# An encoder layer with expert retrieval: the v stage set up two blocks ahead, gathers spread over the whole stage

## The chip, the cores and the metric

One core of one Trainium2 chip. The metric is the device time of one execution in microseconds (us). The engines are named as the profile names them: PE is TensorE (with PEld for its weight loads), DVE is VectorE, ACT is ScalarE, POOL is GpSimd, and SP is SyncE, whose instruction stream here holds almost nothing but DMA issues (SPq). Each engine works through its own instructions strictly in order.

## The reference

One encoder layer, run on two sequences that share the weights: a prompt of 256 tokens and a sample of 512 tokens, model width 1024. After a norm and a projection come a banded attention and a dilated attention, gated, merged and added to x. Then follows the expert layer, where the change is:

```python
def peer(h, w_query, sub_keys_1, sub_keys_2, expert_u, expert_v):
    ...
    v1, i1 = lax.top_k(s1, PEER_TOPK)
    v2, i2 = lax.top_k(s2, PEER_TOPK)
    ...
    idx = (e1 * PEER_KEYS + e2).reshape(T, PEER_HEADS * PEER_TOPK)
    g = jax.nn.softmax(top, axis=-1).reshape(T, PEER_HEADS * PEER_TOPK)
    ...
        u = expert_u[ic]
        a = jax.nn.gelu(jnp.einsum('ted,td->te', u, tc, preferred_element_type=jnp.float32), approximate=False)
        vv = expert_v[ic]
        return jnp.einsum('te,ted->td', (gc * a).astype(tc.dtype), vv)
```

Each token picks 128 of 16384 experts (8 heads, 16 each) with gate weights g. A chosen expert gives gelu(u . h) times its gate, and that many times its row of expert_v is added to x. All is float32.

## The kernel before

**Products.** A float32 operand is split into two parts in the fast matmul format: `split` (L138) writes hi, a cast on ACT (L139), and lo = src - hi, a subtraction on DVE (L140). `mm3` (L143) then makes three matmuls: hi x hi (L144), lo x hi (L145), hi x lo (L146).

**The sample's expert layer is computed densely**, over all 16384 experts in 128 blocks of 128. `gbuild` builds the matrix of gates from one-hot products and stores it to gd in DRAM. The **u stage** (`stage1`, L730) loads a block of expert_u (ur, 512 KB), splits it into uh and ul, makes 24 matmuls against the 512 tokens (tTh, tTl) into pu, applies gelu on ACT (ga_) and stores that (256 KB, issued by ACT) to ad in DRAM. It runs woven into `gbuild`. The **v stage** (`dense`, L743) runs after it: per block, `stage2` (L748) issues on SP the load of vr (a block of expert_v, 512 KB) and of gl (the block's gelu, 256 KB), and for every eighth block gt (gates of eight blocks, 2 MB); it splits vr into vh and vl, multiplies gl by gt on DVE (L761) and splits that into ph and pl. The block's 24 matmuls add into eight banks, held0 to held7 (two halves of four token tiles), which collect over all 128 blocks. Block 122 also loads xe, the residual (2 MB, L774); after the last block each bank is added to xe on DVE (L782) and stored to y (L783).

**The prompt's expert layer is gathered.** `gather` (L790) makes, for each of two tiles of 128 tokens, 128 indirect DMAs of rows of expert_u (512 KB each, issued by POOL, L799, into buffers gr), each with a product and sum against the token on DVE (L806), then 128 of expert_v, each added into x on DVE by its weight (L814): 512 gathers in all. The second tile's x is x5, stored to y (L815) when its last sum is done.

**The order.** The program is written as generators that are woven together: `fill` and `weave` (L818, L827) run one step of the gathers whenever the main work has collected enough "due"; the paces are GB in the build stage and GV in the v stage, in gathers per unit (a block of the v stage yields 0.5 twice). A gather carries a wait called "pace" on `anchor[0]`, the cast or gelu on ACT that was issued last when it was written. From this program a scheduler, which plans with a timeline of its own, sets a fixed order on each engine. Tiles come from pools with a set number of buffers (bufs); a new tile in a buffer waits for the readers of the tile that was there. The pool of the v stage (L842 and below, named dv, from the right side of the memory) is opened when the u stage's pool is closed, and may take its place; then its first tiles wait for what used that memory.

Of the kernel before, what the change touches and what calls it, by code (L numbers as in the profile page):

```python
# [30 lines left out]
SYNC = mybir.DependencyInfo(mybir.DependencyClass.Sync, mybir.DependencyReason.DATA)  # L31
FILL = 2.25
# [12 lines left out]
GB, GV = (2.4, 2.0)  # L45
# [3 lines left out]
def tile_peer(ctx: ExitStack, tc: tile.TileContext, a: dict):  # L49
# [93 lines left out]
    def mm3(out, lh, ll, rh, rl, first, last):  # L143
        pe.matmul(out, lhsT=lh, rhs=rh, start=first, stop=False)  # L144
        pe.matmul(out, lhsT=lh, rhs=rl, start=False, stop=False)  # L145
        pe.matmul(out, lhsT=ll, rhs=rh, start=False, stop=last)  # L146
# [596 lines left out]
    def dense(pv_, psd):  # L743
# [4 lines left out]
        def stage2(j):  # L748
            g, b = divmod(j, GRP)
            if b == 0:  # L750
                gts[g] = pv_.tile([128, S_S // GCH, GRP, GCH], F32, tag="gt", name="gt", bufs=2)
                nc.sync.dma_start(gts[g], gd[:, :, g * GRP:(g + 1) * GRP, :].rearrange("c p e t -> p c e t"))
            vr = pv_.tile([128, D], F32, tag="vr", name="vr", bufs=5)
            nc.sync.dma_start(vr, vrows[j])
            ga = pv_.tile([128, S_S], F32, tag="gl", name="gl", bufs=4)
            nc.sync.dma_start(ga, ad[j])
            vh = pv_.tile([128, D], F32R, tag="vh", name="vh", bufs=3)
            vl = pv_.tile([128, D], F32R, tag="vl", name="vl", bufs=3)
            split(vh, vl, vr)
            gv = ga.rearrange("p (c t) -> p c t", t=GCH)  # L760
            ve.tensor_tensor(gv, gv, gts[g][:, :, b, :], op=ALU.mult)  # L761
            ph = pv_.tile([128, S_S], F32R, tag="ph", name="ph", bufs=3)
            pl = pv_.tile([128, S_S], F32R, tag="pl", name="pl", bufs=3)
            anchor[0] = split(ph, pl, ga)
            return ph, pl, vh, vl

        nxt = stage2(0)
        for j in range(128):
            ph, pl, vh, vl = nxt
            if j < 127:  # L770
                nxt = stage2(j + 1)
# [4 lines left out]
            for i in range(8):  # L776
# [3 lines left out]
                mm3(held[i], ph[:, c], pl[:, c], vh[:, cs], vl[:, cs], j == 0, j == 127)  # L780
                if j == 127:
                    ve.tensor_tensor(x[t][:, cs], held[i], x[t][:, cs], op=ALU.add)  # L782
                    nc.sync.dma_start(a["y"][t * 128:(t + 1) * 128, cs], x[t][:, cs])  # L783
# [180 lines left out]
```

## Time and profile before

| what | value |
|---|---|
| time, three runs | 2470.12, 2473.23, 2475.72 us (median 2473.23) |
| profiled execution, device time | 2468.71 us |
| its span | 2466.9 us |
| PE busy | 2350.8 us (95%), 11926 matmuls |
| PEld busy | 1964.5 us (80%) |
| DVE busy | 1886.5 us (76%) |
| ACT busy | 1076.1 us (44%) |
| POOL busy | 812.1 us (33%) |
| DMA | 642.79 MB, mean 261 GB/s |

The span is the stretch of the trace; the device time holds 1.8 us around it. Times in the rows are in us from the start of the span. The u stage ends at about 1725 us and the v stage fills the rest. A matmul row has a modelled end, so matmuls are best counted by their starts. In a row of the windows the engines come in the order PE, PEld, DVE, ACT, POOL, and PEclk is the granted clock of PE as a share of full speed. In a timeline row the value in brackets is how long the engine had been idle before, and what released it.

### The profile page before, as it was taken

To read this page: it belongs to the slowest core of one execution; us is meant where nothing else is said; L and a number is where in the kernel's file an instruction comes from. 1 tells how busy PE (TensorE), PEld (TensorE's weight loads), DVE (VectorE), ACT (ScalarE), POOL (GpSimd) and SP (SyncE) were. 2 spreads that over 40 slices of the span, in tenths; PEclk is the share of its full clock that TensorE was granted. 3 is DMA by queue.
4 is the path that set the end of the run, shared out by engine and by line. 5 is a ranking of instruction groups with operands and counts; after the bars stand their busy time and mean duration, and the time that the engine had idled before them with its cause. 6 is when DMAs were issued, how large, how long until landed. Compare 5 with 4: busy or idle time off the path is not lost. (4 is left out here: it accounts for less than half of the span.)

```text
span 2466.9 us, 34172 instructions
## 1 busy us (share of the span) xinstructions
PE 2350.8 (95%) x11926; PEld 1964.5 (80%) x11926; DVE 1886.5 (76%) x4013; ACT 1076.1 (44%) x1848; POOL 812.1 (33%) x624
## 2 busy tenths in 40 slices
PE   8998998999998999999999999997999999999999
PEld 6787877877887888888888888876888777777777
DVE  6765699677688889978579889853787888789873
ACT  5764435434433344367466666732222222222222
POOL 0000320345555401044144544420444443444310
PEclk9999999989998999999999999999999999999999
DMA  6423542467787434479789999995899999999972
GB/s 214 145 87 128 179 136 73 151 224 224 271 280 262 137 107 137 152 289 370 250 305 372 358 352 341 339 375 211 322 392 368 343 349 352 356 353 371 376 268 103
DMA packets 246365, 642.79 MB, mean 261 GB/s; under 512 B 22576, under 2 KB 77488, under 8 KB 244144
## 3 DMA queue, kind: packets, MB, share of 16 engines
q1 hardware_dynamic: 151728, 305.02, 36.4%
q0 software_dynamic: 73728, 268.47, 30.0%
q10 hardware_dynamic: 20736, 67.12, 6.8%
q8 instruction: 94, 1.54, 0.3%
q14 instruction: 79, 0.65, 0.1%
HBM read 561.60 MB, written 77.59 MB: 259 GB/s over the span
## 5 line engine op out<-in xcount | busy, mean ns | idle before, releaser
L799 POOL DMA_INDIRECT gr<-u,pidx x256 | 329.0, 1285 | 558.9 <-ACT ph L139 168.1
L799 POOL DMA_INDIRECT gr<-v,pidx x256 | 333.4, 1302 | 459.9 <-ACT ph L139 196.2
L144 PE MATMUL held<-vh,ph 128*128 128x512 f32 x1024 | 403.0, 394 | 31.3 <-ACT ph L139 30.7
L144 PE MATMUL pu<-tTh,uh 128*128 128x512 f32 x1024 | 407.4, 398 | 14.2 <-ACT uh L139 14.2
L146 PE MATMUL pu<-tTh,ul 128*128 128x512 f32 x1024 | 401.3, 392 | 4.1 <-DVE ul L140 4.1
L806 DVE SCALAR_TENSOR_TENSOR gr<-gr,tok 128x1024 f32<-128x1024 f32 x256 | 330.8, 1301 | 96.7 <-DMA gr<-u,pidx 96.5
L145 PE MATMUL held<-vl,ph 128*128 128x512 f32 x1024 | 400.8, 391 | 0.0
L145 PE MATMUL pu<-tTl,uh 128*128 128x512 f32 x1024 | 400.6, 391 | 0.0
L814 DVE SCALAR_TENSOR_TENSOR x<-gr,act,x 128x1024 f32<-128x1024 f32 x256 | 327.4, 1279 | 42.5 <-DMA gr<-v,pidx 40.6
L146 PE MATMUL held<-vh,pl 128*128 128x512 f32 x1024 | 314.9, 389 | 0.0
L144 PEld LDWEIGHTS held<-vh,ph 128*128 128x128 f32 x1024 | 193.9, 189 | 78.3 <-ACT ph L139 37.2
L140 POOL TENSOR_TENSOR wlo<-wraw,whi 128x1024 fp32r<-128x1024 f32 x51 | 128.6, 2522 | 376.8 <-ACT whi L139 373.8
L139 ACT CAST vh<-vr 128x1024 fp32r<-128x1024 f32 x128 | 134.5, 1051 | 257.0 <-PE held L146 154.2
L144 PEld LDWEIGHTS pu<-tTh,uh 128*128 128x128 f32 x1024 | 193.8, 189 | 53.2 <-ACT uh L139 15.9
L140 DVE TENSOR_TENSOR vl<-vr,vh 128x1024 fp32r<-128x1024 f32 x128 | 156.5, 1222 | 102.4 <-ACT vh L139 98.4
L146 PEld LDWEIGHTS pu<-tTh,ul 128*128 128x128 f32 x1024 | 193.3, 189 | 46.2 <-DVE ul L140 6.1
L145 PEld LDWEIGHTS held<-vl,ph 128*128 128x128 f32 x1024 | 193.8, 189 | 40.0
L146 PEld LDWEIGHTS held<-vh,pl 128*128 128x128 f32 x1024 | 192.2, 188 | 40.0
L145 PEld LDWEIGHTS pu<-tTl,uh 128*128 128x128 f32 x1024 | 193.5, 189 | 37.6
L139 ACT CAST whi<-wraw 128x1024 fp32r<-128x1024 f32 x137 | 143.8, 1050 | 167.7 <-DMA wraw<-w_in 52.7
L139 ACT CAST uh<-ur 128x1024 fp32r<-128x1024 f32 x128 | 133.8, 1050 | 175.7 <-PE pu L145 92.7
L139 ACT CAST ph<-gl 128x512 fp32r<-128x512 f32 x128 | 79.4, 620 | 267.0 <-DVE gl L761 106.5
(400 smaller groups left out, 4565.5 us busy)
## 6 DMA issues: line engine op xcount, KB each, us to landing
ur<-ublk SPq DMA_DIRECT2D x128, 512.0 KB
vr<-v SPq DMA_DIRECT2D x128, 512.0 KB
wraw<-w_in SPq DMA_DIRECT2D x80, 512.0 KB
gd<-gs ACTq DMA_DIRECT2D x16, 2048.0 KB
gt<-gd SPq DMA_DIRECT2D x16, 2048.0 KB
gl<-ad SPq DMA_DIRECT2D x128, 256.0 KB
wraw<-w_query SPq DMA_DIRECT2D x32, 512.0 KB
wraw<-w_out SPq DMA_DIRECT2D x16, 512.0 KB
```

The lines of the kernel that those rows point to most:

```text
L139: i = ac.copy(hi, src)
L140: eng.tensor_tensor(lo, src, hi.bitcast(F32), op=ALU.subtract)
L144: pe.matmul(out, lhsT=lh, rhs=rh, start=first, stop=False)
L145: pe.matmul(out, lhsT=lh, rhs=rl, start=False, stop=False)
L146: pe.matmul(out, lhsT=ll, rhs=rh, start=False, stop=last)
L799: st = gp.indirect_dma_start(out=g, out_offset=None, in_=tab, in_offset=bass.IndirectOffsetOnAxis(ap=pidx[t][:, s:s + 1], axis=0))
L806: ve.scalar_tensor_tensor(g, g, 1.0, tok, op0=ALU.mult, op1=ALU.mult, accum_out=act[:, s:s + 1])
L814: ve.scalar_tensor_tensor(xt, g, act[:, s:s + 1], xt, op0=ALU.mult, op1=ALU.add)
```

## The change

`stage2` is called two blocks ahead of the matmuls instead of one: the parts of blocks 0 and 1 are set up first, then in turn block j+2 before the matmuls of block j. vh, vl, ph and pl have four buffers each instead of three, vr has four instead of five. GB goes from 2.4 to 2.3 and GV from 2.0 to 1.75. In the last block each bank's three matmuls are tied to come behind those of the bank before (a dependency that sets the scheduler's order and puts no wait into the program). Line numbers shift by one to seven.

```diff
--- before.py
+++ after.py
@@ -29,6 +29,7 @@
 CAND = [16 // (i + 1) for i in range(16)]
 NCAND = sum(CAND)
 SYNC = mybir.DependencyInfo(mybir.DependencyClass.Sync, mybir.DependencyReason.DATA)
+ORDERED = mybir.DependencyInfo(mybir.DependencyClass.NoSync, mybir.DependencyReason.DATA)
 FILL = 2.25
 FG = 2.25
 FL = {"p": 1, "s": 3}
@@ -42,7 +43,7 @@
 PGP, PGS = (0.5, 0.45)
 ORDER, SLB = ('pppbpbbb', 3)
 U0, UP, UB = (8, 0.45, 1.0)
-GB, GV = (2.4, 2.0)
+GB, GV = (2.3, 1.75)
 
 
 @with_exitstack
@@ -141,9 +142,10 @@
         return i
 
     def mm3(out, lh, ll, rh, rl, first, last):
-        pe.matmul(out, lhsT=lh, rhs=rh, start=first, stop=False)
-        pe.matmul(out, lhsT=lh, rhs=rl, start=False, stop=False)
-        pe.matmul(out, lhsT=ll, rhs=rh, start=False, stop=last)
+        a_ = pe.matmul(out, lhsT=lh, rhs=rh, start=first, stop=False)
+        b_ = pe.matmul(out, lhsT=lh, rhs=rl, start=False, stop=False)
+        c_ = pe.matmul(out, lhsT=ll, rhs=rh, start=False, stop=last)
+        return a_, b_, c_
 
     def norm_tok(pool, xt, g, dst, ssq=None):
 
@@ -750,25 +752,26 @@
             if b == 0:
                 gts[g] = pv_.tile([128, S_S // GCH, GRP, GCH], F32, tag="gt", name="gt", bufs=2)
                 nc.sync.dma_start(gts[g], gd[:, :, g * GRP:(g + 1) * GRP, :].rearrange("c p e t -> p c e t"))
-            vr = pv_.tile([128, D], F32, tag="vr", name="vr", bufs=5)
+            vr = pv_.tile([128, D], F32, tag="vr", name="vr", bufs=4)
             nc.sync.dma_start(vr, vrows[j])
             ga = pv_.tile([128, S_S], F32, tag="gl", name="gl", bufs=4)
             nc.sync.dma_start(ga, ad[j])
-            vh = pv_.tile([128, D], F32R, tag="vh", name="vh", bufs=3)
-            vl = pv_.tile([128, D], F32R, tag="vl", name="vl", bufs=3)
+            vh = pv_.tile([128, D], F32R, tag="vh", name="vh", bufs=4)
+            vl = pv_.tile([128, D], F32R, tag="vl", name="vl", bufs=4)
             split(vh, vl, vr)
             gv = ga.rearrange("p (c t) -> p c t", t=GCH)
             ve.tensor_tensor(gv, gv, gts[g][:, :, b, :], op=ALU.mult)
-            ph = pv_.tile([128, S_S], F32R, tag="ph", name="ph", bufs=3)
-            pl = pv_.tile([128, S_S], F32R, tag="pl", name="pl", bufs=3)
+            ph = pv_.tile([128, S_S], F32R, tag="ph", name="ph", bufs=4)
+            pl = pv_.tile([128, S_S], F32R, tag="pl", name="pl", bufs=4)
             anchor[0] = split(ph, pl, ga)
             return ph, pl, vh, vl
 
-        nxt = stage2(0)
+        nxt = [stage2(0), stage2(1)]
+        prev = None
         for j in range(128):
-            ph, pl, vh, vl = nxt
-            if j < 127:
-                nxt = stage2(j + 1)
+            ph, pl, vh, vl = nxt.pop(0)
+            if j < 126:
+                nxt.append(stage2(j + 2))
             if j == 122:
                 xe = pv_.tile([128, 4, D], F32, tag="gt", name="xe", bufs=2)
                 nc.sync.dma_start(xe, xs.rearrange("(t p) d -> p t d", p=128))
@@ -777,8 +780,12 @@
                 t, n = divmod(i, 2)
                 c = slice(t * 128, t * 128 + 128)
                 cs = slice(n * 512, n * 512 + 512)
-                mm3(held[i], ph[:, c], pl[:, c], vh[:, cs], vl[:, cs], j == 0, j == 127)
+                ms = mm3(held[i], ph[:, c], pl[:, c], vh[:, cs], vl[:, cs], j == 0, j == 127)
                 if j == 127:
+                    if prev is not None:
+                        for m in ms:
+                            tc.add_manual_dep(m.ins, prev.ins.name, ORDERED, reason="output by output")
+                    prev = ms[2]
                     ve.tensor_tensor(x[t][:, cs], held[i], x[t][:, cs], op=ALU.add)
                     nc.sync.dma_start(a["y"][t * 128:(t + 1) * 128, cs], x[t][:, cs])
                 if i % 4 == 3:
```

How the instructions stand then on the engines, at three places.

**ACT, v stage, blocks 81 to 86 of before.** vh and ph are the casts of split; the numbers only tell tiles apart. In the order of blocks these rows are ph81, vh83, ph82, vh84, vh85, ph83, vh86, ph84, ph85:

```order
L139 CAST ph_20132<-gl_20125 128x512
L139 CAST vh_20213<-vr_20209 128x1024
L139 CAST ph_20175<-gl_20168 128x512
L139 CAST vh_20256<-vr_20252 128x1024
L139 CAST vh_20299<-vr_20295 128x1024
L139 CAST ph_20218<-gl_20211 128x512
L139 CAST vh_20342<-vr_20338 128x1024
L139 CAST ph_20261<-gl_20254 128x512
L139 CAST ph_20304<-gl_20297 128x512
```

The same place after; in the order of blocks vh81, ph81, vh82, vh83, vh84, ph82, ph83, ph84, vh85, ph85:

```order
L140 CAST vh_20013<-vr_20009 128x1024
L140 CAST ph_20018<-gl_20011 128x512
L140 CAST vh_20056<-vr_20052 128x1024
L140 CAST vh_20096<-vr_20092 128x1024
L140 CAST vh_20139<-vr_20135 128x1024
L140 CAST ph_20061<-gl_20054 128x512
L140 CAST ph_20101<-gl_20094 128x512
L140 CAST ph_20144<-gl_20137 128x512
L140 CAST vh_20182<-vr_20178 128x1024
L140 CAST ph_20187<-gl_20180 128x512
```

Before, vh85 stands ahead of ph83 and vh86 ahead of ph84: two blocks ahead, with three buffers. After, three vh stand in a row, then three ph; vh84 stands two blocks ahead of ph82, with four buffers, and no vh stands three blocks ahead of a ph.

**SP, from the u stage to the v stage, before.** ur is a block of the u stage, gt, vr and gl are the loads of the v stage; behind a row stands what it waits for (DMAHW and DMASW are transfers, the others engines):

```order
L732 DMA ur_16314<-ublk 128x1024 [waits DMAHW0_49,DVE_49]
L752 DMA gt_16641<-gd_91 128x16x256 [waits DMAHW5_49,DMAHW1_49,PE_49]
L754 DMA vr_16643<-v 128x1024 [waits DMAHW6_49]
L756 DMA gl_16645<-ad_95 128x512 [waits PE_49]
L754 DMA vr_16656<-v 128x1024
L756 DMA gl_16658<-ad_95 128x512 [waits DMASW4_49,DMASW5_49,DMASW3_49,DMASW6_49,DMASW2_49,DMASW7_49,DMASW1_49,DMAHW1_49,DMASW0_49,DVE_49]
L754 DMA vr_16699<-v 128x1024 [waits DMAHW3_49]
```

Six more ur, down to that of block 127, stand further down this queue, behind thirteen more loads of the v stage. After:

```order
L734 DMA ur_16494<-ublk 128x1024 [waits DMAHW3_49,DVE_49]
L734 DMA ur_16528<-ublk 128x1024 [waits DMAHW4_49,DVE_49]
L734 DMA ur_16562<-ublk 128x1024 [waits DMAHW6_49,DMAHW2_49,DVE_49]
L754 DMA gt_16617<-gd_91 128x16x256 [waits DMAHW4_49,DMAHW5_49,DMAHW3_49,DMAHW6_49,DMAHW1_49,DMAHW7_49,DMAHW0_49,Activation_49]
L756 DMA vr_16619<-v 128x1024 [waits DMAHW2_49]
L758 DMA gl_16621<-ad_95 128x512
L756 DMA vr_16632<-v 128x1024
L758 DMA gl_16634<-ad_95 128x512
```

The last ur stands ahead of every load of the v stage now, and the first gt waits for eight semaphores: the last gelu of the u stage (ga_ of block 127) and the last seven stores of ga_ to ad. The v stage's pool is 8 KB per partition larger, and the first gt now lies on the memory of ga_.

**DVE, at the end of the program, before.** xe is the residual, held3 to held7 the last banks:

```order
L782 TENSOR_TENSOR xe_21887<-held3_16636,xe_21887 128x512
L782 TENSOR_TENSOR xe_21887<-held4_16637,xe_21887 128x512
L782 TENSOR_TENSOR xe_21887<-held5_16638,xe_21887 128x512
L782 TENSOR_TENSOR xe_21887<-held6_16639,xe_21887 128x512
L782 TENSOR_TENSOR xe_21887<-held7_16640,xe_21887 128x512
L955 UNCONDITIONAL_BRANCH
```

After (x5 is the sum of the prompt's second token tile, gr a gather; behind the last row stand eight more of its kind, then the branch that ends the program):

```order
L789 TENSOR_TENSOR xe_21848<-held2_16611,xe_21848 128x512
L821 SCALAR_TENSOR_TENSOR x5_81<-gr_21920,act_15363,x5_81 128x1024
L789 TENSOR_TENSOR xe_21848<-held3_16612,xe_21848 128x512
L789 TENSOR_TENSOR xe_21848<-held4_16613,xe_21848 128x512
L789 TENSOR_TENSOR xe_21848<-held5_16614,xe_21848 128x512
L789 TENSOR_TENSOR xe_21848<-held6_16615,xe_21848 128x512
L821 SCALAR_TENSOR_TENSOR x5_81<-gr_21960,act_15363,x5_81 128x1024
L789 TENSOR_TENSOR xe_21848<-held7_16616,xe_21848 128x512
L821 SCALAR_TENSOR_TENSOR x5_81<-gr_21988,act_15363,x5_81 128x1024
L821 SCALAR_TENSOR_TENSOR x5_81<-gr_22003,act_15363,x5_81 128x1024
L821 SCALAR_TENSOR_TENSOR x5_81<-gr_22018,act_15363,x5_81 128x1024
```

Before, all sums of gathers are done ahead of the additions; after, two sums stand between the additions and twelve behind the last one.

## Rows read from the trace of the kernel before

**Rows 1.** Windows: stretch, length, engines' busy us (count), PEclk, DMA share, GB/s.

```profile
1500.00:1600.00 100.00, 100.00 (x547) 86.43 (x547) 85.17 (x140) 72.49 (x134) 42.67 (x33) 1.00 0.92 343
...
1726.00:1958.00 232.00, 232.00 (x1024) 192.16 (x1025) 181.27 (x265) 66.21 (x82) 106.48 (x80) 1.00 0.97 358
1958.00:2363.00 405.00, 378.03 (x1645) 308.27 (x1644) 332.26 (x365) 113.60 (x140) 167.16 (x137) 1.00 0.97 356
```

**Rows 2.** Waits of PE from 1600 us: engine, line, releaser; total us, times, longest.

```profile
PE held L144 <- ACT ph L139: 30.7, 15, 4.9
PE pu L144 <- ACT uh L139: 13.5, 3, 9.7
```

**Rows 3.** Timeline, a v stage wait: start, us, engine, line, operation, [idle <-releaser].

```profile
2203.78 1.98 PE L146 MATMUL held<-vh,pl 128*128 128x512 f32 x8
2205.84 1.04 ACT L139 CAST vh<-vr 128x1024 fp32r<-128x1024 f32 x1 [5.87 <-issue]
2206.79 0.61 ACT L139 CAST ph<-gl 128x512 fp32r<-128x512 f32 x1
2206.91 1.22 DVE L140 TENSOR_TENSOR vl<-vr,vh 128x1024 fp32r<-128x1024 f32 x1 [1.25 <-ACT vh L139]
2207.45 0.50 PE L144 MATMUL held<-vh,ph 128*128 128x512 f32 x1 [1.70 <-ACT ph L139]
```

**Rows 4.** Timeline, end of u stage, first matmul of the v stage.

```profile
1625.51 0.39 PE L146 MATMUL pu<-tTh,ul 128*128 128x512 f32 x1
...
1672.93 1.04 ACT L139 CAST vh<-vr 128x1024 fp32r<-128x1024 f32 x1 [4.70 <-DMA gt<-gd]
...
1675.49 0.79 PE L144 MATMUL pu<-tTh,uh 128*128 128x512 f32 x1 [9.66 <-ACT uh L139]
...
1724.77 0.39 PE L146 MATMUL pu<-tTh,ul 128*128 128x512 f32 x1
1725.85 0.50 PE L144 MATMUL held<-vh,ph 128*128 128x512 f32 x1 [0.69 <-ACT ga__16617 L740]
```

**Rows 5.** Timeline, PE right after its waits at 1628 and 1630.

```profile
1631.35 0.63 PE L144 MATMUL pu<-tTh,uh 128*128 128x512 f32 x1
1631.78 0.63 PE L145 MATMUL pu<-tTl,uh 128*128 128x512 f32 x1
```

**Rows 6.** Timeline, issues of loads and stores, and first uses of loads.

```profile
1643.62 0.54 SPq L752 DMA_DIRECT2D gt<-gd  x1
...
1658.35 0.69 DVE L761 TENSOR_TENSOR gl<-gl,gt 128x512 f32<-128x512 f32 x1 [4.36 <-DMA gl<-ad]
...
1725.82 0.33 ACTq L741 DMA_DIRECT2D ad<-ga__16617  x1
...
2399.61 0.37 SPq L774 DMA_DIRECT2D xe<-xs  x1
...
2408.74 0.32 SPq L756 DMA_DIRECT2D gl<-ad  x1
...
2411.46 0.69 DVE L761 TENSOR_TENSOR gl<-gl,gt 128x512 f32<-128x512 f32 x1 [0.79 <-DMA gl<-ad]
```

**Rows 7.** Timeline, sums of gathers next to other DVE work, and PE's last matmul.

```profile
2350.20 1.28 DVE L814 SCALAR_TENSOR_TENSOR x<-gr,act,x 128x1024 f32<-128x1024 f32 x1
2351.40 1.22 DVE L140 TENSOR_TENSOR vl<-vr,vh 128x1024 fp32r<-128x1024 f32 x1
...
2380.06 1.23 DVE L140 TENSOR_TENSOR vl<-vr,vh 128x1024 fp32r<-128x1024 f32 x1 [3.57 <-ACT vh L139]
2381.20 2.60 DVE L814 SCALAR_TENSOR_TENSOR x<-gr,act,x 128x1024 f32<-128x1024 f32 x2
...
2461.52 0.39 PE L146 MATMUL held<-vh,pl 128*128 128x512 f32 x1
```

**Rows 8.** Waits of DVE from 1700 us, for loads of gl.

```profile
DVE gl L761 <- DMA gl<-ad: 18.1, 6, 8.3
```

**Rows 9.** DMA from 2395 to 2415 us, in 40 slices of 0.5 us.

```profile
GB/s 0 0 0 0 0 0 33 197 291 21 205 287 229 229 352 401 410 401 401 418 418 426 418 430 385 414 410 385 180 57 225 242 0 115 311 352 229 41 0 0
```

## The prediction

> **What bounds the kernel now.** I read the busy times by stage first [rows 1], then what TensorE (PE) waited for [rows 2], then one of those waits matmul by matmul [rows 3], then the change from the u stage to the v stage [rows 4 to 6]. Up to 1600 us and again from 1726 to 1958 PE is busy all the time at a granted clock of 1.00: 1024 matmuls in 232 us, 0.2267 us each, so a block of 24 is 5.44 us. Time is lost only where PE runs dry, and from 1600 on that happens in two places.
>
> In the v stage 3071 matmul steps lie between the first start at 1725.85 and the last at 2461.52 [rows 4, 7]. They need 696.1 us and took 735.7: 39.6 us lost. All fifteen waits there end on ScalarE (ACT), on ph [rows 2], and rows 3 show one of thirteen that are alike. PE finishes block 83 at about 2203.78 + 8 x 0.2267 = 2205.59. Only then does ACT start a vh, at 2205.84, then ph, which ends at 2207.40, and PE starts at 2207.45: 1.86 us after it could have. The order says why: ACT holds vh of block j+2 ahead of ph of block j. With three vh buffers that vh waits until block j-1 has been used up, and the ph that PE needs next stands behind it. In the order of before a vh stands two ahead of a ph for exactly fifteen blocks (43, 44, 47, 51, 59, 67, 68, 75, 83, 84, 91, 99, 107, 111, 115): the fifteen waits. Thirteen at 1.86 make 24.2 us; the other two are longer (4.89 us the longest) and are followed by matmuls at half clock.
>
> In the end of the u stage, blocks 114 to 127 are 336 steps, 76.2 us; from 1625.51 to 1724.77 they took 99.3 [rows 4]: 23.1 us lost. The longest wait (9.66 us) is a cast of uh that stood on ACT behind a vh of the v stage, which waited for its transfer until 1672.93 [rows 4]. The order has uh directly behind the gelu of the block before it (so that PE must run dry) for blocks 114, 120 and 122 here, and in no other block from 109 on.
>
> **The change, part by part**, against the profiled execution's own time (span 2466.9, device time 2468.7, which is 4.5 below the median of 2473.2).
>
> *Set-up two ahead, four buffers.* vh of block k now waits for block k-4. In the new ACT order no vh stands three ahead of a ph, which is what it would take to repeat the stall. Where ACT groups blocks (vh82, vh83, vh84, ph82, ph83, ph84), vh84 waits for the end of block 80, and ph82 is needed one whole block, 5.44 us, later. The longest chain into it that the order has is vh, vl, one gather's sum, gl, ph: 0.25 + 1.07 + 1.14 to 1.22 + 1.20 to 1.30 + 0.77 + 0.66 = 5.1 to 5.3 us (vh to vl and ph to PE from rows 3, vl and the sum by rows 3 and 7, gl 0.69 and a hand-over of 0.08). It fits by 0.2 to 0.35 us, in two groups (88 and 112); everywhere else gl stands ahead of that sum or of vl, with over 1.5 us to spare. vr has four buffers instead of five, which brings its load nearer to its use, from about 25 to about 19 us; loads now hardly end a wait (all gl loads together 18.1 us on VectorE (DVE), none on PE [rows 2, 8]). So I take all 39.6 us as gone; if a few groups slip, 25 are.
>
> *Room.* The same four buffers make the pool of the v stage 8 KB per partition larger (vr -4, vh and vl +4 each, ph and pl +2 each). Before, it lay above the u stage's tiles; now it starts at byte 105408, and its lowest tile, the first gt, lies on ga_ (105984 to 112128). That is the wait list on gt in the order: the last gelu and the last seven stores to ad. SP's queue is in order, so vr, gl and all else of the v stage stand behind it. Two things follow.
>
> First, nothing of the v stage can stand among the last uh any more, and in the new order every uh has at least two blocks of lead on ACT. The u stage's 23.1 us should go (-23.1; -15 if some uh still comes late).
>
> Second, the v stage starts cold. Let Z be the time at which PE could go on (1724.77 + 0.23 = 1725.0 before). The store of the last ga_ is issued at Z + 0.8 [rows 6]. No row shows how long a store takes to land. A 256 KB load takes 2.72 us from issue to use (2408.74 to 2411.46 [rows 6]), so gt is issued at Z + 3.5. Then gt, vr0 and gl0, 2.75 MB, come through one queue. A load of that size (xe, with a vr and a gl) was issued from 2399.61 on and moved at 350 to 430 GB/s until about 2409.3 [rows 6, 9]: 9.7 us. That gives Z + 13.2, and with gl 0.69 and ph to PE 0.66 [rows 3] Z + 14.6, against Z + 0.85 before: +13.7. The far ends are 7 us (all bytes at 410 GB/s with no latency) and 14.7 us (the first gt before, 1643.62 to 1658.35, with all else in flight [rows 6]): +11 to +19. After a wait this long PE also restarts slow: after the pair of waits at 1628 and 1630 the matmuls are 0.43 us apart instead of 0.23 [rows 5], for some 14 of them, +2.8. Sum of the start: +16.5. By the Trainium skill, DMA: Bandwidth & Descriptors, section "Anatomy of one DMA — SWDGE (gpsimd) path", a transfer that POOL issues costs about 2.0 us plus its bytes at 436 GB/s. The 2.72 us row, of one that SP issues, agrees with it (2.6); by it the three would take 8.6 us (estimate), and the sum would be 1.1 us lower.
>
> *Gathers.* 282 instead of 290 are issued before the v stage, leaving 230 instead of 222, and at 1.75 per block they don't fit: the last are set after block 127. PE is full in the build stage anyway [rows 1], so eight fewer there are worth nothing. What they cost is the end. In the order of DVE one gather's sum now stands ahead of the last of the eight additions, and twelve behind it. Sums in a row into the same x take 2.60 us for two [rows 7], so 13 x 1.30 = 16.9 us. The gathers themselves are released by ph127, about 15 us before the last matmul, so their data are there, two excepted, which wait for a buffer until the last block and land in time. The last store is then y of 512 KB instead of 256 KB, +0.7. Together +17.6 (from +14, if sums overlap as between other work, to +22). Before, the sums were done 80 us early and the end was the additions' own.
>
> *Last block output by output.* The order of before already had it so; the new dependency keeps it. Worth 0.
>
> **Sum:** -39.6 - 23.1 + 16.5 + 17.6 = -28.6 us. 2468.7 - 28.6 = 2440.1 for the profiled execution; against the median, 2473.2 - 28.6 = 2444.6.
>
> **Rivals.**
> *The transfers become the bound.* Per block 1.05 MB of vr, gl and gt and 1.75 x 0.52 MB of gathers; with xe and 218 gathers that is 251 MB until PE's end. At the 356 to 358 GB/s of rows 1 this is 702 us, just inside the 707 us from Z + 5.6 on that the sum gives PE. Against it: 0.97 share is not full, and slices reach 430 [rows 9]. It decides below 354 GB/s; at 343 (the lowest full window, rows 1) it adds 23 us. At 350, +9: 2454; I hold 2445 to 2467. Chance 0.14.
> *The start is hidden or cheap:* gt's wait comes early enough, as it did before. Then 13 of the 16.5 us stay away: 2431. Against it: the wait names the last gelu. Chance 0.07.
> *The u stage keeps part of its waits,* by ur's two buffers and the sums ahead of ul: +8 to +20, so 2453 to 2464. Chance 0.08.
> *Slower: the groups of four stall.* From block 22 on the order has 27 groups. If gathers come so late that the sum between vl and gl passes the 5.44 us of the chain above, each group head costs a stall like that of rows 3: 27 x 1.86 = 50 us, 2495. It decides when a gather takes over 15 us from its release to its sum. Against it: the order has each sum four blocks or more behind its release, as before, and only the u gathers ever waited. Chance 0.06.
>
> **How the numbers follow.** Forecast 2444 us, chance 0.65. The range 2429 to 2467 takes in the forecast's own bounds (start +11 to +19, end +14 to +22, up to 15 us of stalls left), the transfers, the cheap start and most of the late u stage; it leaves out the slower case and the far ends, under 2 in 10. A measurement of this kernel tells about 0.2%, 5 us, from no change. Faster by more 0.90, within 0.04 (the transfers at their worst), slower 0.06.
>
> **What would show it.** In the profile after: PE's waits on ph in the v stage gone, or one at the group heads; no PE wait on uh after 1600 us; one PE gap of some 14 us between the last pu and the first held matmul, with SP's gt issued after the last gelu, then matmuls 0.43 us apart; a v stage of about 700 us from first to last matmul; then twelve sums of 1.3 us behind the last addition, and y as the last transfer. It is wrong if the v stage takes over 715 us (then the waits name a DMA, or a gather's sum), if the gap at its start is under 5 or over 20 us, or if the end is the additions.

## The result

The changed kernel took 2440.75 us (median of four runs, 2436.87 to 2441.63) beside 2474.18 for the kernel before: a ratio of 0.9873, interval 0.9853 to 0.9892. In a second set of runs it took 2438.92 beside 2464.72, 0.9883 (0.9845 to 0.9921). 2444 was forecast. The profiled execution has a span of 2439.8 us, 27.1 less than before; 28.6 less was the sum of the prediction.

Busy times by stage, after (stretch, length, then PE, PEld, DVE, ACT and POOL with counts, PEclk, DMA share, GB/s); they answer to [rows 1]:

```profile
1600.00:1701.00 101.00, 101.00 (x473) 84.28 (x472) 41.41 (x61) 34.71 (x48) 17.71 (x13) 1.00 0.62 231
1701.00:1718.50 17.50, 0.02 (x1) 0.00 (x0) 1.40 (x2) 2.27 (x4) 0.00 (x0) 0.56 0.81 273
1718.50:1726.40 7.90, 7.86 (x25) 6.30 (x26) 7.90 (x11) 4.70 (x6) 3.01 (x1) 0.69 1.08 365
1726.40:1958.00 231.60, 231.60 (x1023) 191.81 (x1022) 181.85 (x268) 69.55 (x85) 89.49 (x76) 1.00 0.98 367
1958.00:2363.00 405.00, 405.00 (x1788) 335.18 (x1788) 329.30 (x383) 118.73 (x148) 169.19 (x129) 1.00 0.97 360
2417.00:2440.00 23.00, 0.53 (x3) 0.11 (x1) 18.57 (x17) 0.00 (x0) 1.88 (x2) 0.56 0.56 223
```

PE is busy in all of the end of the u stage and in all of the v stage. What is new is the stretch of 17.5 us with almost nothing in it, a slow start of 7.9 us behind it (granted clock 0.69 on average), and 23 us at the end in which DVE works alone. All waits of PE from 1600 us on, the answer to [rows 2], are one row:

```profile
PE held L145 <- ACT ph L140: 17.5, 1, 17.5
```

The change of stages, after (a timeline; in brackets the idle time before and what ended it), which answers to [rows 4, 6]:

```profile
1700.63 0.39 PE L147 MATMUL pu<-tTh,ul 128*128 128x512 f32 x1
1701.05 0.60 ACT L742 ACTIVATE ga__16593<-pu 128x512 f32<-128x512 f32 x1 [4.84 <-PE pu L147]
1701.68 0.33 ACTq L743 DMA_DIRECT2D ad<-ga__16593  x1
1703.72 0.38 SPq L754 DMA_DIRECT2D gt<-gd  x1
1704.15 1.99 SPq L756 DMA_DIRECT2D vr<-v  x1
...
1716.36 1.04 ACT L140 CAST vh<-vr 128x1024 fp32r<-128x1024 f32 x1 [14.71 <-DMA vr<-v]
1717.10 0.69 DVE L763 TENSOR_TENSOR gl<-gl,gt 128x512 f32<-128x512 f32 x1 [35.72 <-DMA gl<-ad]
1717.87 0.62 ACT L140 CAST ph<-gl 128x512 fp32r<-128x512 f32 x1 [0.46 <-DVE gl L763]
1718.54 0.80 PE L145 MATMUL held<-vh,ph 128*128 128x512 f32 x1 [17.52 <-ACT ph L140]
```

The last matmul of the u stage starts at 1700.63, the first of the v stage at 1718.54. Between them stand the last gelu, its store, then gt, issued 2.04 us after that store, and then the transfers: the first vr is there at 1716.36, the first gl and gt at 1717.10.

The end, after, which answers to [rows 7]:

```profile
2417.15 0.39 PE L147 MATMUL held<-vh,pl 128*128 128x512 f32 x1
2419.56 0.68 DVE L789 TENSOR_TENSOR xe<-held,xe 128x512 f32<-128x512 f32 x1
2420.16 15.80 DVE L821 SCALAR_TENSOR_TENSOR x<-gr,act,x 128x1024 f32<-128x1024 f32 x12
2435.99 0.33 SPq L823 DMA_DIRECT2D y<-x  x1
```

The last addition starts at 2419.56; twelve sums follow it, and y of the prompt's second tile is stored at 2435.99.

Term by term, from the starts of matmuls in both profiles:

| term | predicted, us | in the profiles, us |
|---|---|---|
| before the end of the u stage | 0 | -1.0 |
| end of the u stage, blocks 114 to 127 | -23.1 | -23.1 |
| last u matmul to first v matmul | +13.7 | +16.8 |
| slow matmuls after it | +2.8 | +2.4 |
| waits in the v stage | -39.6 | -39.5 |
| last matmul to the end of the span | +17.6 | +17.3 |
| sum | -28.6 | -27.1 |

The second row is the time lost there, 99.27 - 76.2 us before and nothing after. The last blocks of the changed kernel also hold 1.8 us of the build stage's matmuls, which are counted in the first row. The v stage, from its first matmul to its last, went from 735.67 to 698.61 us, of which 696.1 are its 3071 steps and 2.4 the slow start. The first row is within what executions differ by: the first gelu of the u stage came at 890.39 and 894.70 us in two of the changed kernel. The bounds set in the prediction (v stage over 715 us, gap under 5 or over 20) were kept, and the end is the sums and not the additions.

### The profile page after: what moved, and what is told of

Its sections match the earlier page's. It is cut to its first block, busy times and chain, and to the rows that moved or that the text cites. A ratio compares the mean times of both kernels' runs of the same rounds, so it can differ in the third digit from the quotient of the medians.

```text
span 2439.8 us, 34171 instructions
## 1 busy us (share of the span) xinstructions
PE 2332.6 (96%) x11926; PEld 1958.4 (80%) x11926; DVE 1880.8 (77%) x4013; ACT 1073.6 (44%) x1848; POOL 830.0 (34%) x624
## 4 chain that ended last, share of the span: by engine, by line
PE 77%; DMA 8%; DVE 7%; issue 3%; ACT 2%; POOL 2%; SPq 0%; POOLq 0%; ACTq 0%; DVEq 0%
PE held L145 10%; PE held L146 9%; PE held L147 9%; PE pu L147 9%; PE pu L146 9%; PE pu L145 9%; PE p_g L725 5%; DMA wraw<-w_in 3%; DMA gr<-u,pidx 2%; PE pg L245 1%; PE pg L244 1%; DVE wlo L141 1%; POOL wlo L141 1%; PE pg L243 1%; ACT whi L140 1%
## 5 line engine op out<-in xcount | busy, mean ns | idle before, releaser
L806 POOL DMA_INDIRECT gr<-v,pidx x256 | 353.4, 1381 | 462.6 <-ACT ph L140 187.7
L145 PE MATMUL held<-vh,ph 128*128 128x512 f32 x1024 | 399.1, 391 | 17.5 <-ACT ph L140 17.5
L147 PE MATMUL held<-vh,pl 128*128 128x512 f32 x1024 | 332.4, 389 | 0.0
```

The source lines that it names most:

```text
L145: a_ = pe.matmul(out, lhsT=lh, rhs=rh, start=first, stop=False)
L147: c_ = pe.matmul(out, lhsT=ll, rhs=rh, start=False, stop=last)
L806: st = gp.indirect_dma_start(out=g, out_offset=None, in_=tab, in_offset=bass.IndirectOffsetOnAxis(ap=pidx[t][:, s:s + 1], axis=0))
```

## The experiments

From the trace of each: the time from the gelu of u block 113 to that of block 127 (76.2 us are 14 blocks of matmuls; in all kernels but before, e3_bufs and e10_room_early 16 matmuls of the build stage stand among them, which makes 77.96 without any loss), the start of the last u matmul to the first v matmul, the first to the last v matmul (696.1 without any loss), the last matmul to the end. Then the median time, and its ratio to the kernel before on the same chip with its interval.

| kernel | u end | gap | v stage | end | median | ratio |
|---|---|---|---|---|---|---|
| before | 99.27 | 1.08 | 735.67 | 5.38 | 2474.18 | |
| after | 77.95 | 17.91 | 698.61 | 22.65 | 2440.75 | 0.9873 (0.9853 to 0.9892) |
| e9_after_again | 77.96 | 18.98 | 699.25 | 22.66 | 2438.92 | 0.9883 (0.9845 to 0.9921) |
| e1_room | 77.96 | 3.35 | 697.79 | 22.71 | 2428.61 | 0.9831 (0.9794 to 0.9868) |
| e2_pace195 | 77.96 | 17.53 | 697.97 | 5.16 | 2426.62 | 0.9826 (0.9787 to 0.9866) |
| e3_bufs | 82.93 | 16.74 | 698.98 | 5.09 | 2431.43 | 0.9846 (0.9811 to 0.9881) |
| e4_noorder | 77.96 | 18.70 | 698.73 | 23.19 | 2443.15 | 0.9900 (0.9861 to 0.9939) |
| e5_room_pace195 | 77.96 | 3.34 | 700.29 | 4.94 | 2408.57 | 0.9757 (0.9725 to 0.9789) |
| e6_pace_alone | 93.80 | 1.08 | 710.19 | 18.55 | 2450.64 | 0.9936 (0.9913 to 0.9958) |
| e7_lead_alone | 92.47 | 1.07 | 711.59 | 22.46 | 2456.43 | 0.9938 (0.9908 to 0.9968) |
| e8_first_gt_4k | 77.96 | 14.34 | 699.19 | 22.66 | 2434.62, one run | |
| e10_room_early | 76.16 | 3.34 | 699.07 | 5.03 | 2413.17 | 0.9770 (0.9728 to 0.9812) |
| e11_gt_1k_near | 77.95 | 14.83 | 699.09 | 24.99 | 2440.61, one run | |
| e12_gt_4k_far | 77.96 | 14.99 | 698.26 | 24.97 | 2441.20, one run | |

The runs were made on several chips, so medians are compared through the ratios. The intervals of e1_room, e2_pace195 and e3_bufs still touch that of the changed kernel: what one edit was worth is read from the stages.

**The cold start: is it the place of gt?** In e1_room one line of stage2 moves, so that pl and not gt lies on the memory of ga_:

```diff
             g, b = divmod(j, GRP)
+            pl = pv_.tile([128, S_S], F32R, tag="pl", name="pl", bufs=4)
             if b == 0:
...
             ph = pv_.tile([128, S_S], F32R, tag="ph", name="ph", bufs=4)
-            pl = pv_.tile([128, S_S], F32R, tag="pl", name="pl", bufs=4)
```

> The changed kernel with one line moved: pl's tile is made ahead of gt's, so that the lowest tiles of the v stage's pool, the ones on the memory of ga_, are pl's four and no longer gt's first. Nothing else is changed; gt, vr and gl can then be issued behind the last ur, and only the first write of pl waits for the last stores to ad. Theory (the 17.9 us gap of PE between the stages is gt's wait for the last gelu and its stores, and then the transfer of gt, vr and gl in the open): the gap falls to 2 to 5 us, the slow matmuls after it mostly go, and the time is 12 to 17 us below that of the changed kernel, 2424 to 2429. Rival (the gap is the stage's own, from the casts and the product that must follow the last gelu): the gap stays over 12 us and the time within 5 us of the changed kernel. Both: end of the kernel unchanged, 22.6 us from the last matmul to the end.

The gap fell from 17.91 to 3.35 us, and nothing else in the table moved by 1 us. Its timeline at the change of stages:

```profile
1676.37 0.38 SPq L755 DMA_DIRECT2D gt<-gd  x1
...
1705.58 0.60 ACT L742 ACTIVATE ga__16593<-pu 128x512 f32<-128x512 f32 x1 [4.84 <-PE pu L147]
1706.88 1.04 ACT L140 CAST vh<-vr 128x1024 fp32r<-128x1024 f32 x1 [0.70 <-ACT ga__16593 L742]
1707.83 0.61 ACT L140 CAST ph<-gl 128x512 fp32r<-128x512 f32 x1
1708.50 0.79 PE L145 MATMUL held<-vh,ph 128*128 128x512 f32 x1 [2.96 <-ACT ph L140]
```

gt is issued 29 us ahead of the last gelu. What is left of the gap is the casts that must follow that gelu on ACT: vh, then ph. The rival is out.

**The end: is it the pace?** e2_pace195 changes one number:

```diff
-GB, GV = (2.3, 1.75)
+GB, GV = (2.3, 1.95)
```

> The changed kernel with a pace of 1.95 gathers per block in the v stage in place of 1.75, and nothing else. In its order the last gather is released at block 119, all sums stand ahead of the additions, and vh stands at most one block ahead of ph. Theory (the end of the changed kernel is twelve sums and a store behind the last addition, and its v stage has no other loss): 22.6 us from the last matmul to the end become 5 to 6, the v stage stays at about 699 us from first to last matmul, and the time is 2422 to 2426. Rival (the transfers bound the v stage, and the slow pace is what let PE run full): at 2.07 MB per block 1.95 asks for 381 GB/s where the changed kernel has moved 359 to 367, so the v stage gets longer by 10 to 25 us, with PE waiting for ph behind a late gather's sum or a late load, and the time comes to 2433 or more.

The end fell from 22.65 to 5.16 us and the v stage lost 1.9 us, the slow start. Its windows over the v stage:

```profile
1723.60:1958.00 234.40, 234.40 (x1026) 194.01 (x1027) 193.85 (x287) 71.44 (x89) 101.06 (x83) 0.99 1.01 385
1958.00:2363.00 405.00, 405.00 (x1788) 335.52 (x1787) 348.43 (x395) 118.95 (x149) 183.18 (x145) 1.00 1.01 381
```

The rival's premise was wrong: 381 to 385 GB/s went through, with PE busy all the time. All eight additions stand together at the end again:

```profile
2417.21 5.45 DVE L789 TENSOR_TENSOR xe<-held,xe 128x512 f32<-128x512 f32 x8 [12.02 <-PE held L147]
```

**The fifteen waits: buffers or lead?** e3_bufs puts the buffers of the change into the kernel before; e7_lead_alone takes them out of the changed kernel and leaves the rest.

```diff
-            vr = pv_.tile([128, D], F32, tag="vr", name="vr", bufs=5)
+            vr = pv_.tile([128, D], F32, tag="vr", name="vr", bufs=4)
...
-            vh = pv_.tile([128, D], F32R, tag="vh", name="vh", bufs=3)
+            vh = pv_.tile([128, D], F32R, tag="vh", name="vh", bufs=4)
...
```

(for e3_bufs; vl, ph and pl as vh. e7_lead_alone is the reverse of it in the changed kernel.)

> The kernel before with the buffers alone of the change: four of vh, vl, ph and pl, four of vr; set-up one block ahead, paces and last block as before. Theory (what removes the fifteen waits is the fourth buffer, and the larger pool on the memory of ga_ is what clears the end of the u stage and makes the cold start, whatever the lead): no wait of PE on ph in the v stage but the first; a gap of about 18 us between the stages; end as before, 5 us from the last matmul. Time 2474 - 39.6 - 22 + 19 = 2431, within 2425 to 2437. Rival (the second block of lead is what removes the waits): the v stage still has ten or more waits of PE on ph, and the time is 2450 or more.

> The changed kernel with the buffers of before: three of vh, vl, ph and pl, five of vr; two blocks ahead, paces and last block as changed. In its order vh stands two blocks ahead of ph for seven blocks (77, 83, 91, 99, 107, 117, 123), and eleven sums stand behind the last addition. Theory (the lead in the program text is worth nothing by itself, the buffers decide): seven waits of PE on ph, 13 us lost in the v stage; 8 to 16 us lost at the end of the u stage; gap 1 to 2 us; 20 to 22 us at the end. Time 2474 - 26.5 - 11 + 16 = 2452, within 2445 to 2459. Rival (the lead of two removes the waits whatever the buffers): under 4 us lost in the v stage and 2443 or less.

Waits of PE from 1600 us on in e3_bufs, total us, times, longest:

```profile
PE held L144 <- ACT ph L139: 16.4, 1, 16.4
PE pu L144 <- ACT uh L139: 2.2, 1, 2.2
PE pu L146 <- DVE ul L140: 1.7, 1, 1.7
```

The one wait on ph is the cold start; the v stage took 698.98 us, with a lead of one block. In e7_lead_alone, with a lead of two and three buffers:

```profile
PE pu L145 <- ACT uh L140: 12.5, 1, 12.5
PE held L145 <- ACT ph L140: 12.2, 7, 2.0
```

Seven waits, for the seven blocks that the order names, and 711.59 us. The buffers removed the waits; the lead alone did not. But e3_bufs has another order, too: no vh stands ahead of the ph of an earlier block in it, so by the rule of the prediction it would not have waited with three buffers either. That the fourth buffer itself does it is seen in the changed kernel, where vh stands two ahead of ph for twelve blocks and none of them waits.

By its stages (end of the u stage without the build stage's 1.8 us, gap, v stage, end) e3_bufs takes 803.7 us, the whole change 815.3: by these stages, what it has beside the buffers cost more than it brought. The intervals of the two ratios overlap.

**The paces alone,** in the kernel before:

```diff
-GB, GV = (2.4, 2.0)
+GB, GV = (2.3, 1.75)
```

> The kernel before with the two paces of the change (2.3 and 1.75) and nothing else. In its order vh stands two blocks ahead of ph for seven blocks (83, 84, 92, 99, 108, 115, 124) where the kernel before has fifteen, uh stands directly behind the gelu of the block before it for block 120 only, six casts of the v stage still stand ahead of the last gelu, and nine sums stand behind the last addition. Theory (a wait for each block where vh stands as many blocks ahead of ph as there are buffers less one; each sum behind the last addition costs 1.3 us): seven waits of PE on ph, 13 us lost in the v stage for 39.5; 8 to 16 us lost at the end of the u stage for 23; gap 1 us; 18 to 19 us from the last matmul to the end. Time 2474 - 26.5 - 11 + 13.5 = 2450, within 2443 to 2457. Rival (the waits come from the gathers' rate and not from the casts' order): the v stage loses under 5 or over 25 us.

```profile
PE pu L144 <- ACT uh L139: 12.6, 1, 12.6
PE held L144 <- ACT ph L139: 11.9, 7, 1.7
```

Again as many waits as the order has such blocks (seven), 14 us lost for the 13 expected. So part of what looked like the work of the buffers (fifteen waits to seven) comes with another order, which the paces alone already give. The end grew to 18.55 us. The u stage still lost 15.8 us (93.80 - 77.96), as expected, and most of it at one place:

```profile
1649.03 0.43 SPq L752 DMA_DIRECT2D gt<-gd  x1
1650.00 7.29 SPq L732 DMA_DIRECT2D ur<-ublk  x2
...
1665.93 1.04 ACT L139 CAST uh<-ur 128x1024 fp32r<-128x1024 f32 x1 [6.05 <-DMA ur<-ublk]
...
1667.03 0.79 PE L144 MATMUL pu<-tTh,uh 128*128 128x512 f32 x1 [12.61 <-ACT uh L139]
...
1668.26 12.26 SPq L732 DMA_DIRECT2D ur<-ublk  x4
```

PE waits 12.61 us for uh, uh waits for its load ur, and ur stands on SP right behind gt and other loads of the v stage: issued from 1650.00 on, it is used at 1665.93. The last four ur are issued behind more of them, from 1668.26 on.

**The tie in the last block.** e4_noorder:

```diff
                 if j == 127:
-                    if prev is not None:
-                        for m in ms:
-                            tc.add_manual_dep(m.ins, prev.ins.name, ORDERED, reason="output by output")
-                    prev = ms[2]
...
```

> The changed kernel without the dependency that ties the banks of the last block to one another. Theory (the banks stood one behind the other already, so the tie is worth nothing): the same time as the changed kernel within 2 us, 2439 to 2443. Rival (without the tie the scheduler weaves the last block's banks, and the additions and stores of y come later): 1 to 4 us slower.

Without the tie the order has the first five banks woven: their matmuls of hi x hi and lo x hi first, then five of hi x lo, so that the first addition comes late. It costs half a microsecond at the end here (23.19 for 22.65), where twelve sums follow anyway. The medians (2443.15, and 2440.75 and 2438.92 in other sets of runs) are not told apart: the intervals of the ratios overlap. That run is inconclusive on the time; the stages say under 1 us.

> The changed kernel once more, as the measure for the two kernels that are compared with it on other chips, e4_noorder and e5_room_pace195. Theory (the kernels differ by what their stages show, the rest is the chip): a ratio to the kernel before of 0.985 to 0.990, gap 17.5 to 18.5, v stage 698 to 699, 22 to 23 us from the last matmul to the end. Were e4_noorder really slower, this run would have a ratio under 0.985.

The ratio came as expected; the gap was 18.98 us, half a microsecond over.

**Why the start took 16.8 and not 13.7 us.** Three kernels load the first gt from another place and are else the changed kernel:

```diff
-                nc.sync.dma_start(gts[g], gd[:, :, g * GRP:(g + 1) * GRP, :].rearrange("c p e t -> p c e t"))
+                if g == 0:
+                    nc.sync.dma_start(gts[g].rearrange("p c e t -> p (c e t)").rearrange("p (t d) -> p t d", d=D), xs.rearrange("(t p) d -> p t d", p=128))
+                else:
+                    nc.sync.dma_start(gts[g], gd[:, :, g * GRP:(g + 1) * GRP, :].rearrange("c p e t -> p c e t"))
```

(e8_first_gt_4k; the other two differ from it in the view that is loaded.)

> The changed kernel with the first load of gt taken from xs instead of gd: the same 2 MB into the same tile behind the same waits, but in pieces of 4 KB instead of 1 KB. The gates of the first eight blocks are therefore not the reference's; the work is the same. Theory (the first gt is slow because of its small pieces; a load of xe in 4 KB pieces was the measure in the prediction): first vh 3 to 4 us earlier after the issue of gt, gap 14 to 15 us in place of 17.9. Rival (the queue starts slowly whatever it carries, or the vr and gl behind it are what takes long): gap 17 us or more.

> The changed kernel with the first load of gt taken from xs in pieces of 1 KB that stand 1 KB apart from partition to partition and 128 KB apart within a partition; gd has pieces of 1 KB that stand 16 KB and 2 MB apart. The gates of the first eight blocks are not the reference's; the work is the same. Theory (the size of the pieces made the first gt slow): 12 to 13.5 us from the issue of gt to the first vh, a gap of 17 to 19 us, as in the changed kernel. Rival (the distance between the pieces did): 9 to 10 us and a gap of 14 to 15 us, as in e8_first_gt_4k.

> The changed kernel with the first load of gt taken from gd in pieces of 4 KB, four per partition, still 16 KB apart from partition to partition and 2 MB apart within a partition. The gates of the first eight blocks are not the reference's; the work is the same. Theory (the size of the pieces): 9 to 10 us from the issue of gt to the first vh, a gap of 14 to 15 us. Rival (the distance): 12 us or more and a gap of 17 us or more.

Issue of gt and first vh in each, first e8_first_gt_4k, which took 9.09 us:

```profile
1699.70 0.38 SPq L755 DMA_DIRECT2D gt<-xs  x1
...
1708.79 1.04 ACT L140 CAST vh<-vr 128x1024 fp32r<-128x1024 f32 x1 [11.15 <-DMA vr<-v]
```

e11_gt_1k_near, 9.57 us:

```profile
1702.97 0.38 SPq L755 DMA_DIRECT2D gt<-xs  x1
...
1712.54 1.04 ACT L140 CAST vh<-vr 128x1024 fp32r<-128x1024 f32 x1 [11.63 <-DMA vr<-v]
```

e12_gt_4k_far, 9.72 us:

```profile
1704.26 0.38 SPq L755 DMA_DIRECT2D gt<-gd  x1
...
1713.98 1.04 ACT L140 CAST vh<-vr 128x1024 fp32r<-128x1024 f32 x1 [11.78 <-DMA vr<-v]
```

The changed kernel took 12.64 us (1703.72 to 1716.36). The same load, behind the same waits, took 13.71 in e9_after_again, 13.44 in e4_noorder, 12.26 in e2_pace195 and 11.48 in e3_bufs. The three kernels with other pieces lie below all five. So e11_gt_1k_near came as its rival had it and e12_gt_4k_far as its theory had it: neither the size of the pieces nor their distance is enough, and both together (1 KB pieces, 16 KB and 2 MB apart) took 2.4 to 4.6 us more than the 9.09. The three themselves are single runs and differ by 0.5 to 0.6 us, less than the 2.2 us between the five executions of one load, and are not told apart. What in the memory makes the two work together was not tried. e8_first_gt_4k and e11_gt_1k_near also read another tensor (xs); 1 KB pieces close together from gd were not tried. The Trainium skill, DMA: Bandwidth & Descriptors, section "Latency and other measured facts", says that a row pitch of a large power of two (2 MiB among them) slows copies down; that pitch is from one partition's row to the next, which is 16 KB in gd, so no run here shows it. (The ends of e11 and e12 are 2.3 us longer than that of the changed kernel; that was not followed up.)

**Both remedies at once.** e5_room_pace195 joins e1 and e2:

> The changed kernel with both edits that helped alone: pl's tile made ahead of gt's (as in e1_room) and 1.95 gathers per block in the v stage (as in e2_pace195). Theory (the gap at the start and the sums at the end are two separate costs of the change): gap 3 to 4 us, v stage 698 us, 5 us from the last matmul to the end; against the changed kernel 14.6 and 17.4 us less, 2406 to 2412, a ratio to the kernel before of 0.974. Rival (both are one supply of transfers: starting warm at the faster pace brings gathers and loads into each other's way): the v stage loses 10 us or more and the time stays over 2418.

2408.57 us beside 2466.57, a ratio of 0.9757; by the ratios some 30 us less than the changed kernel. The two costs add up as separate ones do: gap 3.34, end 4.94. The v stage has 4.1 us of loss where 1.8 was expected. PE waited for ph twice, 4.5 us in all. The vh that began the second wait:

```profile
1757.80 1.05 ACT L140 CAST vh<-vr 128x1024 fp32r<-128x1024 f32 x1 [10.40 <-DMA vr<-v]
```

The second wait, of 1.5 us, is at block 11, where no vh stands early: that block's vh waited 10.40 us for its load, and two products of gathers stood between vl and gl on DVE. The granted clock then fell to 0.5 from 1765.2 to 1768.6. A late load is what the rival had named; it cost under 4 us and not 10. This is the fastest kernel of the study.

**More gathers ahead instead of a faster pace.** e10_room_early:

```diff
-GB, GV = (2.3, 1.75)
+GB, GV = (2.6, 1.75)
```

with pl as in e1_room.

> The changed kernel with pl's tile made ahead of gt's (as in e1_room) and the paces 2.6 and 1.75 in place of 2.3 and 1.75: twenty more gathers are issued ahead of the v stage, 210 are left for it and the last is released at block 121, so that the v stage keeps the slow pace and still ends with the additions. Theory (what made the end long is the count left over, not the pace itself): gap 3 to 4 us, v stage 697 to 699, 5 us at the end, as in e5_room_pace195; uh stands directly behind the gelu of the block before for blocks 105 and 108, which costs 0 to 4 us at the end of the u stage: 2406 to 2414. Rival (the build stage has no room for more gathers): its part before the v stage gets 5 us longer or more, and the time is 2415 or more.

Gap, v stage and end came as expected, the time too (2413.17). The u stage got longer in the profiled execution, the slowest of its four (2421.42 us): from its first gelu to its last it took 814.2 us, for 806.0 to 811.6 in nine executions that have the pace of 2.3 and lose nothing at the end of the stage. Nearly all of that is lost at block 108, one of the two places that the expectation had named, where uh stands directly behind a gelu:

```profile
1598.46 1.99 ACT L140 CAST uh<-ur 128x1024 fp32r<-128x1024 f32 x2 [0.45 <-ACT ga__15718 L742]
1599.56 0.50 PE L145 MATMUL pu<-tTh,uh 128*128 128x512 f32 x1 [2.18 <-ACT uh L140]
...
1602.45 0.79 PE L147 MATMUL pu<-tTh,ul 128*128 128x512 f32 x1 [2.16 <-DVE ul L141]
```

With the matmuls behind it at a granted clock of 0.51, 6.3 us were lost there, where 0 to 4 had been expected. Without them the stage took 807.9 us, as long as the others: the runs do not bear out the rival. Whether e10_room_early and e5_room_pace195 differ in time is not settled (the intervals of their ratios overlap).

## Why the prediction came out as it did

**The v stage: right, as argued.** There is a wait for each block where vh stands as many blocks ahead of ph as there are buffers less one. Four kernels bear it out: fifteen such blocks and fifteen waits in the kernel before, seven and seven in e6_pace_alone and e7_lead_alone, none and none in the changed kernel, whose twelve blocks with vh two ahead do not wait. A late load can make a wait, too, as in e5_room_pace195. What removed the waits is the buffers, not the lead: the fourth one in the changed kernel, another order in e3_bufs. The tightest chain was also there, in the two groups that were named. The first of them, in the changed kernel (PE is at the last eight matmuls of block 85, one row):

```profile
2183.87 1.05 ACT L140 CAST vh<-vr 128x1024 fp32r<-128x1024 f32 x1 [4.67 <-PE held L147]
2184.95 1.22 DVE L141 TENSOR_TENSOR vl<-vr,vh 128x1024 fp32r<-128x1024 f32 x1 [4.49 <-ACT vh L140]
2186.09 1.28 DVE L821 SCALAR_TENSOR_TENSOR x<-gr,act,x 128x1024 f32<-128x1024 f32 x1
2186.97 1.98 PE L147 MATMUL held<-vh,pl 128*128 128x512 f32 x8
2187.29 0.69 DVE L763 TENSOR_TENSOR gl<-gl,gt 128x512 f32<-128x512 f32 x1
2188.05 0.62 ACT L140 CAST ph<-gl 128x512 fp32r<-128x512 f32 x1 [3.13 <-DVE gl L763]
2188.72 0.19 PEld L145 LDWEIGHTS held<-vh,ph 128*128 128x128 f32 x1 [0.20 <-ACT ph L140]
2188.79 0.44 PE L145 MATMUL held<-vh,ph 128*128 128x512 f32 x1
```

vh 2183.87, vl 2184.95, a sum 2186.09, gl 2187.29, ph 2188.05 to 2188.67, and PE goes on at 2188.79, where block 85 ends at 2186.97 + 8 x 0.2267 = 2188.78. Measured over all blocks, ph was done 0.12 us ahead of PE's matmul here, and 0.39 us in the other group (0.2 to 0.35 had been worked out); the next smallest is 1.31. Here the weight load of that matmul did wait 0.20 us for ph, so nothing was left in this group, and that it held is in part luck. The slower rival needs all 27 groups to stall, and outside these two 1.3 us or more were left.

**The end of the u stage: right in size, the cause only half.** The 23.1 us are gone. But the step said that gt's wait for the last gelu keeps the v stage out of the last uh. In e1_room gt does not wait and is issued 29 us ahead, and the u stage still loses nothing: in that order all ur stand ahead of gt and all casts of the v stage behind the last gelu. What the runs show is that it goes with the order of loads and casts: where loads of the v stage stand among the ur (17 of them ahead of the last ur in before, e6 and e7) 14.5 to 23.1 us are lost, where all ur stand ahead 0 to 6.7. By the layout, which no trace shows, the pool lies in all of the latter on the memory of ga_ with some tile, and the scheduler then sets this order; why it does was not tried. e3_bufs, with the pace of before, still lost 6.7 us there, so the larger pool's order brings 16.4 of the 23.1; the paces alone (e6) brought 7.3.

**The cold start: right in kind, 3.1 us too small.** The term that was mis-sized is the transfer of gt, vr and gl, taken as 9.7 us from the load of xe: 4 KB pieces that lie close together. In the changed kernel the last of the three, gl, was used 13.38 us after the issue of gt (1703.72 to 1717.10). With pieces like those of xe (e8_first_gt_4k) it was 9.82 us, and the gap 14.34. The far end of that step's range came from a gt itself, 14.7 us. The wait ahead of the transfer was 0.6 us shorter than taken (gt issued 2.86 us after PE ended, not 3.5).

**The end: right, with two small errors that cancel.** 17.3 for 17.6. Twelve sums stand behind the last addition (three in the list of the order and nine more, not eight) and took 15.80 us in one row, 1.32 each. Counted from PE's last matmul, the last store was issued 17.7 us later than before, where 16.9 had been worked out. From its issue to the end of the span it took 3.8 us, and before 4.3, where 0.7 more had been worked out.

**The gathers ahead of the v stage: right.** Eight fewer in the build stage gave nothing: from the first gelu of the u stage to the last, without what was lost at its end, before took 805.7 us, the changed kernel 810.7 and 806.2. Twenty more (e10) took 807.9 without the waits at block 108, which come from where a cast stands in that order.

**The last block: right in time.** The tie keeps what the order of before had, and without it the banks would be woven, but that moves the end by half a microsecond.

**The transfers as the bound: priced wrongly.** The rival took the 356 to 358 GB/s of [rows 1] as a ceiling, though the kernel before had itself moved 361 GB/s from 1100 to 1200 us. The changed kernel moved 360 to 367, and e2_pace195 381 to 385 over more than 630 us. A share of 0.97 was not full. The Trainium skill, DMA: Bandwidth & Descriptors, section "Where 436 GB/s comes from", has about 358 GB/s as the limit that binds between HBM and SBUF, and beside it one measurement of 425. These windows show more than 358, and the measurement decides. The chance of 0.14 stood on a limit that the runs do not have.

## What to carry to other kernels

Count, on the engine that casts, how far one operand's cast runs ahead of the other's, and compare it with the buffers: each place where the distance is the buffers less one is a wait that can be counted before anything runs. When a pool grows, look at which tile now lies on memory that the stage before uses last: let it be one that is written late, not the first load of the queue. And spread side work over a stage only as far as it ends before the stage does; what is left over is paid in full behind the last matmul.

## What was not expected of the hardware

- 2 MB in pieces of 1 KB that lie 16 KB and 2 MB apart, with the vr behind it, took 11.48 to 13.71 us from issue to use in five executions; the same amount in 1 KB pieces close together took 9.57, in 4 KB pieces far apart 9.72, in 4 KB pieces close together 9.09, one execution each.
- The DMA engines moved 381 to 385 GB/s over 639 us beside a full PE (e2_pace195), where 358 had looked full.
- Gaps of the same length did not bring the same start. Windows after a gap of 3.35 us in e1_room and one of 3.34 us in e5_room_pace195 (the last three numbers are granted clock, DMA share and GB/s):

```profile
1708.50:1712.00 3.50, 3.50 (x9) 2.78 (x10) 3.50 (x5) 2.47 (x3) 0.00 (x0) 0.52 0.72 202
```

```profile
1702.10:1705.60 3.50, 3.50 (x15) 2.90 (x16) 3.50 (x5) 2.45 (x3) 0.00 (x0) 1.00 0.77 218
```

In the first the granted clock was 0.52 (the lower level, 1.2 GHz, nearly all the time) and the matmuls lost 1.7 us; in the second it stayed at 1.00 and they lost 0.1. After the gap of 17.91 us in the changed kernel it was 0.50 from 1718.5 to 1722.1, and they lost 2.4.
